# Down blocks of seven: one sum of weight quadrants by a transfer, and the last sums, transfers and two product chains in another order

## The chip, the cores and the metric

The kernel runs on one core of a Trainium2 chip. The metric is the device time of one execution in microseconds (us). The core's engines are TensorE (PE; its weight loads are listed apart as PEld), VectorE (DVE), ScalarE (ACT), GpSimd (POOL) and SyncE (SP). Each works through its own instructions in a fixed order and waits for the others by semaphores. Transfers are issued by SP, ACT or POOL and moved by 16 DMA engines. Matrix products go from SBUF to PSUM, whose banks ACT and DVE empty.

## The reference, cut to what matters

A decoder of two layers over 512 tokens of width 1024. Each layer has a mixing part and then a feed-forward part; only the latter is touched:

```
f = rmsnorm(h, ln_ffn_pre[layer])
f = (silu(f @ w_ffn_gate[layer]) * (f @ w_ffn_up[layer])) @ w_ffn_down[layer]
h = h + rmsnorm(f, ln_ffn_post[layer])
```

`w_ffn_gate` and `w_ffn_up` are 1024 x 2816, `w_ffn_down` is 2816 x 1024, all in f32. The inner width of 2816 is 22 tiles of 128.

## The kernel before, in words

**Three matmuls for one.** An f32 operand is split into a high part (a cast by ACT, `whi`) and a low part (source minus high part, by DVE, `wlo`); both happen in `split`, L239. `mm3` (L191 to L193) multiplies high by high, low by high and high by low into one PSUM bank. So each 128 x 512 piece of a weight costs one ACT and one DVE instruction before PE can use it.

**Seven products for eight.** The feed-forward part multiplies 2 x 2 blocks with seven products instead of eight (the scheme of Strassen and Winograd). The price is sums of quadrants, on DVE, ahead of the splits. `Seven` does it for gate and up: it loads two raw tiles of weights by SP (`loaded`, L144), makes four sums (`sums`, L1041, L1043, L1045, L1046), and seven products of 12 matmuls with 256 columns each, whose results are combined in the tiles x, a (`p`) and e (`q`). Product 7 uses the sum s3 and opens the bank e. `sevens` runs a gate seven and then an up seven, in the order of products 1, 7, 2, 6, 4, 3, 5. Only a layer's first pair goes another way.

**Groups.** After the first two tiles of the inner width (done plainly) come five groups of four: `groups = ((2, 6), (6, 10), (10, 14), (14, 18), (18, 22))`. In a group `sevens` runs twice (tiles m and m + 1 each). The first four groups end in a down block, `down_sevens`; the last one goes to `tail_of`. With two layers there are eight down blocks. PE works through block, gate, up, gate, up, block and so on.

**A down block** multiplies the group's four tiles of activations (two pairs, made by `Inner`, the x of each product) with a 2 x 2 block of `w_down` for each pair. `DownSeven` holds such a block's quadrants a11, a12, a21, a22. The pair's first one (`a` in `down_sevens`) is loaded into two raw tiles (L1194), out of the four that the sevens use too; in each, two quadrants lie side by side, so one quadrant is four pieces of 128 numbers in a partition. The second one (`b`) is spare: it has four tiles of its own (`wd`, L1188), loaded at the start of the second `sevens` of the group. `sums` makes s3 = a11 - a21 (L1205), the parts of a11, a21 + a22 (L1207) and a11 - a21 (L1208), all on DVE; product 3's weight is a further sum (L1220). Each product has 6 matmuls of 512 columns for each of a and b. They go to three pairs of banks: `chain` (tile yc, tag "tr"), `shared` (ys, "lg"), `lows` (yl, "mm"). The order is 1, 7, 2 of a; 1, 7 of b; then product 6 of both into the chain, 2 of b, 5 and 3 of both into the chain, and 4 of both into shared. After product 6 ACT copies the chain's bank into shared (L1256).

**Where the results go.** `ys[tb][dh]` are eight SBUF tiles (token block, half of the output). Some results are copied out by ACT into a tile yo (`put`, L1232) and added to ys by an accumulating transfer from POOL (L1234); some are added by DVE: lows into ys[x][0] (L1262), shared into ys[x][1] (L1265), the chain into ys[x + 2][0] (L1268). ys[x][1] gets one of each, so its sum by DVE waits for the transfer to land. POOL also issues the accumulating transfer that makes some of `Inner`'s low parts (`split_aside`, L1153).

**What sets the order.** The code is written as a flow of tiles. A planner, with its own model of costs, lays down each engine's order ahead of the run: among the instructions that it takes to be ready it picks by their order in the code, `tc.high_priority` raises some, and `tc.issue_after` (in `behind`) ties one behind another on its engine. So an instruction that stands later in the code may be laid ahead of one that stands earlier, but on the chip each engine keeps the order laid down and stands still at an instruction whose input isn't there. Buffers come from pools by tag, and a tile waits for a buffer's last reader.

Of the kernel before, what the change touches and what calls it, by code (L numbers as in the profile page):

```python
# [15 lines left out]
P = 128  # L16
# [24 lines left out]
def hybrid(ctx: ExitStack, tc: tile.TileContext, i: dict, out: bass.AP):  # L41
# [147 lines left out]
    def mm3(o, w, x, start, stop, more=False):  # L189

        PE.matmul(o, w[0], x[0], start=start, stop=False, skip_group_check=more)  # L191
        PE.matmul(o, w[0], x[1], start=False, stop=False, skip_group_check=more)  # L192
        return PE.matmul(o, w[1], x[0], start=False, stop=stop, skip_group_check=more)  # L193
# [891 lines left out]

    ended = [None]

    def sevens(pair, plain_first, opens=False):

        if not plain_first:  # L1090
            for make in pair:
                u = make()
                with behind(ended if opens else ()):
                    u.sums()
                opens = False
                for n in (1, 7, 2, 6, 4, 3, 5):
                    u.run(n)
                u.end()
            return
        us = []  # L1100
        for make in pair:
            us.append(make())
            us[-1].sums()
            for n in (1, 2, 3):
                us[-1].run(n)
        for some in ((7, 6), (4, 5)):
            for u in us:
                for n in some:
                    u.run(n)
        for u in us:  # L1110
            u.end()

    def feed_forward(layer, phase, xp, meanwhile=None):
# [68 lines left out]
        class DownSeven:  # L1182

            def __init__(self, k, spare):
                if spare:
                    self.a = [plain("wd").rearrange("p (m c) -> p m c", m=4) for _ in range(4)]
                    for n, a in enumerate(self.a):
                        last_load[0] = nc.sync.dma_start(  # L1188
                            a, i["w_down"][layer, 4 * (n // 2) : 4 * (n // 2) + 4, :, k + n % 2, :].rearrange("m p c -> p m c"))
                else:  # L1190
                    raws = []
                    for dh in range(2):
                        raw = wp.tile([P, 1024], F32, tag="raw", name=name("raw"), bufs=4)
                        last_load[0] = nc.sync.dma_start(  # L1194
                            raw.rearrange("p (m c) -> p m c", m=4),
                            i["w_down"][layer, 4 * dh : 4 * dh + 4, :, k : k + 2, :].rearrange("m p k c -> p m (k c)"))
                        raws.append(raw.rearrange("p (m k c) -> p m k c", m=4, k=2))
                    self.a = [r[:, :, x, :] for r in raws for x in range(2)]

            def sums(self, pair):  # L1200
                self.x = pair.x
                a11, a12, a21, a22 = self.a
                self.w = {2: a12, 4: a22}
                s3 = temp("s3").rearrange("p (m c) -> p m c", m=4)
                V.tensor_sub(s3, a11, a21)  # L1205
                self.w[1] = self.parts(a11)
                V.tensor_add(a21, a21, a22)  # L1207
                V.tensor_sub(a11, a11, a21)  # L1208
                self.w.update({5: a21, 6: a11, 7: s3})

            def parts(self, src, aside=False):
# [1 line left out]
                split_aside(src, *(t.rearrange("p (m c) -> p m c", m=4) for t in pair), aside)  # L1213
                return pair

            def product(self, outs, n, start, stop):
                w = self.w[n]
                if n == 2:
                    w = self.parts(w)
                    V.tensor_add(self.a[1], self.a[0], self.a[1])  # L1220
                    self.w[3] = self.a[1]
                elif n != 1:
                    w = self.parts(w)
                for x, o in enumerate(outs):
                    c = slice(x * P, (x + 1) * P)
                    mm3(o, tuple(t[:, c] for t in self.x[n]), w, start, stop, True)

        def down_sevens(us, pairs):

            def put(x, *where):  # L1230
                some = prob("yo")
                A.copy(some, x)  # L1232
                for tb, dh in where:
                    G.dma_start(ys[tb][dh], some, accum_op=ALU.add)  # L1234

            def both(outs, n):
                a.product(outs, n, False, False)
                b.product(outs, n, False, True)

            a, b = us  # L1240
            a.sums(pairs[0])
            chain, shared, lows = ([ps(t, s=n) for _ in range(2)] for t, n in (("tr", "yc"), ("lg", "ys"), ("mm", "yl")))
            a.product(chain, 1, True, False)
            a.product(shared, 7, True, False)
            a.product(lows, 2, True, False)
            b.sums(pairs[1])
            b.product(chain, 1, False, True)
            for x in range(2):
                put(chain[x], (x, 0))
            b.product(shared, 7, False, True)  # L1250
            for x in range(2):
                put(shared[x], (x, 1), (x + 2, 1))
            both(chain, 6)
            with tc.high_priority():
                for x in range(2):
                    A.copy(shared[x], chain[x])  # L1256
            b.product(lows, 2, False, True)
            both(chain, 5)
            for x in range(2):
                put(chain[x], (x + 2, 1))  # L1260
            for x in range(2):
                V.tensor_add(ys[x][0], lows[x], ys[x][0])  # L1262
            both(shared, 4)
            for x in range(2):
                V.tensor_add(ys[x][1], shared[x], ys[x][1])  # L1265
            both(chain, 3)
            for x in range(2):
                V.tensor_add(ys[x + 2][0], chain[x], ys[x + 2][0])  # L1268

        fs = [(act("fhi"), act("flo")) for _ in range(2)]  # L1270

# [14 lines left out]
        for tb in range(TB):  # L1286
            for dh in range(2):
# [2 lines left out]
                    token_products(o, fs[k], w[dh][k], tb, k == 0, k == 1)  # L1290
                A.copy(ys[tb][dh], o)

        for gi, (k0, k1) in enumerate(groups):
            fs, pairs, downs = [], [], []
            for m in range(k0, k1, 2):
                if meanwhile and m == k1 - 2 and gi == len(groups) - 1:
                    next(meanwhile)
                if gi < len(groups) - 1:
                    pairs.append(Inner(m < k1 - 2))
                    if m > k0:  # L1300
                        downs.append(DownSeven(m, True))
                else:
                    fs += [(act("fhi"), act("flo")) for _ in range(2)]
                sevens((lambda: Seven(xs, lambda n: i["w_gate"][layer, m + n], "mm", gate_rows),
                        lambda: Seven(xs, lambda n: i["w_up"][layer, m + n], "lg",
                                      lambda row, t: up_rows(row, t, fs, pairs and pairs[-1]))), m == 2, m == k0)
            nk = k1 - k0
            if gi == len(groups) - 1:
                if layer:
# [2 lines left out]
                if meanwhile:  # L1312
# [5 lines left out]
                V.tensor_scalar_mul(eps, eps, RMS_EPS)  # L1318
                return tail_of(fs, lambda kp, dh, aside, k0=k0: down_weights(layer, k0 + 2 * kp, dh, aside), ys, eps,
                               layer == 1)  # L1320
            down_sevens([DownSeven(k0, False)] + downs, pairs)


    def layer_b(phase, fp):
# [297 lines left out]
```

## Time and profile before

| | |
|---|---|
| time, median of 3 runs | 1107.38 us (1104.4 to 1107.46) |
| the profiled execution's time | 1104.82 us |
| its span, first to last instruction | 1103.1 us |
| mean granted clock of PE | 0.998 |
| busy: PE, PEld | 1082.6 us (98%), 983.3 us (89%) |
| busy: DVE, ACT, POOL | 970.7 us (88%), 754.5 us (68%), 93.8 us (9%) |
| DMA queues of SP and of POOL, share of 16 engines | 34.4%, 11.7% |

A line of the profile names engine, line of the code and tiles as output<-inputs, buffer numbers left out. A helper's line stands for all that call it, so L239 is every split; the tile tells them apart. A list of waits says which engine and line waited for which other: us in total, how often, the longest. Matmuls overlap, and one lasts longer (0.28 or 0.39 us) than the step from one start to the next. An event's line can name an earlier wait of its engine.

### The profile page before, as it was taken

To read this page: it belongs to the slowest core of one execution; us is meant where nothing else is said; L and a number is where in the kernel's file an instruction comes from. 1 tells how busy PE (TensorE), PEld (TensorE's weight loads), DVE (VectorE), ACT (ScalarE), POOL (GpSimd) and SP (SyncE) were. 2 spreads that over 40 slices of the span, in tenths; PEclk is the share of its full clock that TensorE was granted. 3 is DMA by queue.
4 is the path that set the end of the run, shared out by engine and by line. 5 is a ranking of instruction groups with operands and counts; after the bars stand their busy time and mean duration, and the time that the engine had idled before them with its cause. 6 is when DMAs were issued, how large, how long until landed. Compare 5 with 4: busy or idle time off the path is not lost.

```text
span 1103.1 us, 19756 instructions
## 1 busy us (share of the span) xinstructions
PE 1082.6 (98%) x7266; PEld 983.3 (89%) x7267; DVE 970.7 (88%) x1942; ACT 754.5 (68%) x1588; POOL 93.8 (9%) x120
## 2 busy tenths in 40 slices
PE   9999999999999999999999999999999999999998
PEld 7998889997979899998988998889997979899996
DVE  7879759998999999997968789868999989999986
ACT  7776578665756757677746788868666756756664
POOL 0000000002020201101000000000002020201100
PEclk9999999999999999999999999999999999999999
DMA  7521331338464664746222654531338464564722
GB/s 269 160 82 51 120 116 39 115 97 191 120 158 125 136 173 97 207 134 193 68 86 59 154 136 120 148 115 40 115 97 191 116 159 129 116 173 106 180 97 77
DMA packets 83992, 139.64 MB, mean 127 GB/s; under 512 B 6772, under 2 KB 49800, under 8 KB 83896
## 3 DMA queue, kind: packets, MB, share of 16 engines
q1 hardware_dynamic: 71480, 116.57, 34.4%
q0 software_dynamic: 11712, 21.50, 11.7%
q8 instruction: 57, 0.93, 0.4%
q10 hardware_dynamic: 704, 0.32, 0.1%
q14 instruction: 39, 0.32, 0.1%
HBM read 105.23 MB, written 2.10 MB: 97 GB/s over the span
## 4 chain that ended last, share of the span: by engine, by line
PE 85%; DVE 5%; DMA 5%; ACT 3%; issue 1%; SPq 1%; POOL 0%; DVEq 0%; ACTq 0%
PE a L193 5%; PE a L192 5%; PE a L191 5%; PE y L191 4%; PE y L193 4%; PE y L192 4%; PE ps L191 4%; PE ps L193 4%; PE ps L192 4%; DMA y<-yo 4%; PE e L193 3%; PE e L192 3%; PE e L191 3%; PE x L193 3%; PE x L192 3%; PE x L191 3%
## 5 line engine op out<-in xcount | busy, mean ns | idle before, releaser
L239 ACT CAST whi<-raw 128x512 fp32r<-128x512 f32 x444 | 260.7, 619 | 117.9 <-DVE raw L1045 58.2
L239 DVE TENSOR_TENSOR wlo<-raw,whi 128x512 fp32r<-128x512 f32 x444 | 290.6, 682 | 21.0 <-ACT whi L239 20.3
L193 PE MATMUL x<-xshi,wlo 128*128 128x256 f32 x320 | 90.4, 282 | 0.2 <-DVE wlo L239 0.2
L192 PE MATMUL x<-xslo,whi 128*128 128x256 f32 x320 | 90.1, 282 | 0.0
L191 PE MATMUL x<-xshi,whi 128*128 128x256 f32 x320 | 90.1, 282 | 0.0
L192 PE MATMUL a<-xslo,whi 128*128 128x256 f32 x320 | 89.9, 281 | 0.0
L191 PE MATMUL a<-xshi,whi 128*128 128x256 f32 x320 | 89.8, 281 | 0.0
L193 PE MATMUL a<-xshi,wlo 128*128 128x256 f32 x320 | 89.7, 281 | 0.0
L1234 POOL DMA_DIRECT2D y<-yo x64 | 55.5, 1143 | 196.9 <-ACT yo L1232 135.0
L191 PE MATMUL ps<-xshi,whi 128*128 128x256 f32 (+1 forms) x224 | 68.4, 306 | 0.0
L192 PE MATMUL ps<-xslo,whi 128*128 128x256 f32 (+1 forms) x224 | 66.7, 298 | 0.0
L193 PE MATMUL ps<-xshi,wlo 128*128 128x256 f32 (+1 forms) x224 | 66.3, 298 | 0.0
L239 ACT CAST whi<-s 128x512 fp32r<-128x512 f32 x56 | 34.7, 620 | 41.0 <-DVE s L1205 25.0
L193 PEld LDWEIGHTS x<-xshi,wlo 128*128 128x128 f32 x320 | 60.6, 189 | 0.4 <-DVE wlo L239 0.4
L191 PEld LDWEIGHTS a<-xshi,whi 128*128 128x128 f32 x320 | 60.2, 188 | 0.4
L192 PEld LDWEIGHTS a<-xslo,whi 128*128 128x128 f32 x320 | 60.2, 188 | 0.4
L192 PEld LDWEIGHTS x<-xslo,whi 128*128 128x128 f32 x320 | 60.5, 189 | 0.0
L191 PEld LDWEIGHTS x<-xshi,whi 128*128 128x128 f32 x320 | 60.5, 189 | 0.0
L193 PEld LDWEIGHTS a<-xshi,wlo 128*128 128x128 f32 x320 | 60.2, 188 | 0.0
L193 PE MATMUL e<-t3hi,wlo 128*128 128x256 f32 x160 | 45.7, 286 | 10.5 <-DVE wlo L239 10.5
L191 PE MATMUL y<-whi,mixedhi 128*128 128x512 f32 x128 | 51.3, 401 | 0.0
L192 PE MATMUL y<-wlo,mixedhi 128*128 128x512 f32 x128 | 50.6, 395 | 0.0
(352 smaller groups left out, 3637.4 us busy)
## 6 DMA issues: line engine op xcount, KB each, us to landing
raw<-in_w_gate SPq DMA_DIRECT2D x44, 512.0 KB, 3.7
raw<-in_w_up SPq DMA_DIRECT2D x44, 512.0 KB, 5.3
y<-yo POOLq DMA_DIRECT2D x64, 256.0 KB, 5.8
raw<-in_w_down SPq DMA_DIRECT2D x28, 512.0 KB, 4.6
raw<-in_w_out SPq DMA_DIRECT2D x16, 512.0 KB, 4.0
wd<-in_w_down SPq DMA_DIRECT2D x32, 256.0 KB, 8.8
flo<-s POOLq DMA_DIRECT2D x16, 256.0 KB, 5.1
raw<-in_w_b_q SPq DMA_DIRECT2D x8, 512.0 KB, 4.4
```

Of the source, the lines that this page charges most:

```text
L191: PE.matmul(o, w[0], x[0], start=start, stop=False, skip_group_check=more)
L192: PE.matmul(o, w[0], x[1], start=False, stop=False, skip_group_check=more)
L193: return PE.matmul(o, w[1], x[0], start=False, stop=stop, skip_group_check=more)
L239: last_parts[:] = A.copy(hi, src), (eng or V).tensor_sub(lo, src, hi)
L1234: G.dma_start(ys[tb][dh], some, accum_op=ALU.add)
```

## The change

It touches `sevens`, `DownSeven`, `down_sevens` and the loop over the groups.

- `DownSeven` issues, when it is made, an accumulating transfer from POOL that adds a22 to a21 inside SBUF. The DVE sum a21 + a22 is gone. s3 is now (a11 - new a21) + a22, made after that difference instead of first.
- The shared results' four transfers into ys go in the order ys[0][1], ys[1][1], ys[2][1], ys[3][1]; before, ys[2][1] was second.
- `both` (products 6, 5, 4, 3) prepares the weights of a and b, then does all matmuls of the first output, a's and b's, and then those of the second. Before, a's for both outputs came first.
- The last sums (the chain into ys[x + 2][0], shared into ys[x][1]) are returned as `rest` and made in the next group's gate seven, behind its product 2.

```diff
--- before.py
+++ after.py
@@ -1085,7 +1085,7 @@
 
     ended = [None]
 
-    def sevens(pair, plain_first, opens=False):
+    def sevens(pair, plain_first, opens=False, rest=None):
 
         if not plain_first:
             for make in pair:
@@ -1095,6 +1095,9 @@
                 opens = False
                 for n in (1, 7, 2, 6, 4, 3, 5):
                     u.run(n)
+                    if rest and n == 2:
+                        rest()
+                        rest = None
                 u.end()
             return
         us = []
@@ -1196,16 +1199,16 @@
                             i["w_down"][layer, 4 * dh : 4 * dh + 4, :, k : k + 2, :].rearrange("m p k c -> p m (k c)"))
                         raws.append(raw.rearrange("p (m k c) -> p m k c", m=4, k=2))
                     self.a = [r[:, :, x, :] for r in raws for x in range(2)]
+                G.dma_start(self.a[2], self.a[3], accum_op=ALU.add)
 
             def sums(self, pair):
                 self.x = pair.x
                 a11, a12, a21, a22 = self.a
                 self.w = {2: a12, 4: a22}
                 s3 = temp("s3").rearrange("p (m c) -> p m c", m=4)
-                V.tensor_sub(s3, a11, a21)
                 self.w[1] = self.parts(a11)
-                V.tensor_add(a21, a21, a22)
                 V.tensor_sub(a11, a11, a21)
+                V.tensor_add(s3, a11, a22)
                 self.w.update({5: a21, 6: a11, 7: s3})
 
             def parts(self, src, aside=False):
@@ -1213,7 +1216,7 @@
                 split_aside(src, *(t.rearrange("p (m c) -> p m c", m=4) for t in pair), aside)
                 return pair
 
-            def product(self, outs, n, start, stop):
+            def weights(self, n):
                 w = self.w[n]
                 if n == 2:
                     w = self.parts(w)
@@ -1221,21 +1224,30 @@
                     self.w[3] = self.a[1]
                 elif n != 1:
                     w = self.parts(w)
+                return w
+
+            def product(self, outs, n, start, stop):
+                w = self.weights(n)
                 for x, o in enumerate(outs):
-                    c = slice(x * P, (x + 1) * P)
-                    mm3(o, tuple(t[:, c] for t in self.x[n]), w, start, stop, True)
+                    self.one(o, x, n, w, start, stop)
+
+            def one(self, o, x, n, w, start, stop):
+                c = slice(x * P, (x + 1) * P)
+                mm3(o, tuple(t[:, c] for t in self.x[n]), w, start, stop, True)
 
         def down_sevens(us, pairs):
 
-            def put(x, *where):
+            def put(x, to):
                 some = prob("yo")
                 A.copy(some, x)
-                for tb, dh in where:
-                    G.dma_start(ys[tb][dh], some, accum_op=ALU.add)
+                G.dma_start(ys[to[0]][to[1]], some, accum_op=ALU.add)
+                return some
 
             def both(outs, n):
-                a.product(outs, n, False, False)
-                b.product(outs, n, False, True)
+                ws = [u.weights(n) for u in us]
+                for x, o in enumerate(outs):
+                    for u, w in zip(us, ws):
+                        u.one(o, x, n, w, False, u is b)
 
             a, b = us
             a.sums(pairs[0])
@@ -1248,8 +1260,9 @@
             for x in range(2):
                 put(chain[x], (x, 0))
             b.product(shared, 7, False, True)
+            both_sums = [put(shared[x], (x, 1)) for x in range(2)]
             for x in range(2):
-                put(shared[x], (x, 1), (x + 2, 1))
+                G.dma_start(ys[x + 2][1], both_sums[x], accum_op=ALU.add)
             both(chain, 6)
             with tc.high_priority():
                 for x in range(2):
@@ -1261,11 +1274,15 @@
             for x in range(2):
                 V.tensor_add(ys[x][0], lows[x], ys[x][0])
             both(shared, 4)
-            for x in range(2):
-                V.tensor_add(ys[x][1], shared[x], ys[x][1])
             both(chain, 3)
-            for x in range(2):
-                V.tensor_add(ys[x + 2][0], chain[x], ys[x + 2][0])
+
+            def rest():
+                for x in range(2):
+                    V.tensor_add(ys[x + 2][0], chain[x], ys[x + 2][0])
+                for x in range(2):
+                    V.tensor_add(ys[x][1], shared[x], ys[x][1])
+
+            return rest
 
         fs = [(act("fhi"), act("flo")) for _ in range(2)]
 
@@ -1290,6 +1307,7 @@
                     token_products(o, fs[k], w[dh][k], tb, k == 0, k == 1)
                 A.copy(ys[tb][dh], o)
 
+        rest = None
         for gi, (k0, k1) in enumerate(groups):
             fs, pairs, downs = [], [], []
             for m in range(k0, k1, 2):
@@ -1303,7 +1321,7 @@
                     fs += [(act("fhi"), act("flo")) for _ in range(2)]
                 sevens((lambda: Seven(xs, lambda n: i["w_gate"][layer, m + n], "mm", gate_rows),
                         lambda: Seven(xs, lambda n: i["w_up"][layer, m + n], "lg",
-                                      lambda row, t: up_rows(row, t, fs, pairs and pairs[-1]))), m == 2, m == k0)
+                                      lambda row, t: up_rows(row, t, fs, pairs and pairs[-1]))), m == 2, m == k0, m == k0 and rest)
             nk = k1 - k0
             if gi == len(groups) - 1:
                 if layer:
@@ -1318,7 +1336,7 @@
                 V.tensor_scalar_mul(eps, eps, RMS_EPS)
                 return tail_of(fs, lambda kp, dh, aside, k0=k0: down_weights(layer, k0 + 2 * kp, dh, aside), ys, eps,
                                layer == 1)
-            down_sevens([DownSeven(k0, False)] + downs, pairs)
+            rest = down_sevens([DownSeven(k0, False)] + downs, pairs)
 
 
     def layer_b(phase, fp):
```

## Prediction

> **What bounds the kernel now.** I read the engine table first, then what TensorE (PE) waits for, then each down block and the stretch behind it by itself, then the order of VectorE (DVE) at one block's end.
>
> The head of the page, then the lists of waits of PE and of DVE (engine, line, what it waited for: us in total, times, longest):
>
> ```profile
> span 1103.1 us, 19756 instructions
> PE 1082.6 (98%) x7266; PEld 983.3 (89%) x7267; DVE 970.7 (88%) x1942; ACT 754.5 (68%) x1588; POOL 93.8 (9%) x120
> ```
> ```profile
> PE e L193 <- DVE wlo L239: 10.5, 6, 2.4
> PE yc L191 <- ACT ys L1256: 2.5, 8, 0.3
> PEld e L193 <- DVE wlo L239: 11.8, 6, 2.6
> PEld yc L191 <- ACT ys L1256: 6.0, 8, 0.8
> DVE y L1265 <- DMA y<-yo: 9.0, 4, 3.5
> DVE y L1265 <- PE yc L193: 6.4, 3, 2.1
> ```
>
> PE is the bound, and little of its time is waiting. Two waits stand out, both at down blocks. Six times, product 7 (tile e) of the gate's first seven behind a block waits for a weight's low part from DVE: 10.5 us by the matmuls, 11.8 by the weight loads. And in each of eight blocks product 5 waits for ACT's copy out of the chain's bank. DVE itself stands 15.4 us ahead of L1265, the sum into ys[x][1].
>
> The stretches show why so small a wait of DVE reaches PE. A block is 20.4 us, what follows up to the next block 41.5 (columns: length, then busy time of PE, PEld, DVE, ACT, POOL, then granted clock, DMA share, GB/s):
>
> ```profile
> 242.10:262.80 20.70, 20.38 (x87) 15.39 (x86) 17.77 (x33) 13.70 (x26) 6.06 (x7) 1.00 0.64 135
> 306.40:326.80 20.40, 20.08 (x87) 15.49 (x85) 17.96 (x33) 13.50 (x26) 6.12 (x7) 1.00 0.64 136
> 326.80:368.30 41.50, 40.02 (x337) 39.81 (x336) 41.35 (x75) 26.59 (x55) 2.58 (x3) 1.00 0.54 150
> 906.40:949.20 42.80, 40.21 (x338) 39.80 (x337) 41.81 (x75) 26.60 (x55) 2.56 (x3) 1.00 0.53 145
> 264.90:267.40 2.50, 0.29 (x4) 0.08 (x2) 2.50 (x6) 2.05 (x5) 0.86 (x1) 1.00 1.13 243
> 268.70:272.10 3.40, 3.40 (x19) 3.40 (x18) 3.40 (x7) 1.20 (x3) 0.00 (x0) 0.50 0.56 161
> ```
>
> Behind the second block (306.4) DVE is busy for 41.35 of 41.5 us: it has no air to make up what it lost. Over that whole group it has 17.96 + 41.35 = 59.3 of 61.9 us, so 2.6 us idle. Where they lie is seen in DVE's timeline at the end of this block, and beside it at the end of the fourth (start, us, instruction, idle before it):
>
> ```profile
> 321.32 0.69 DVE L1041 TENSOR_TENSOR s<-raw,raw 128x512 f32<-128x512 f32 x1
> 321.93 0.69 DVE L239 TENSOR_TENSOR wlo<-raw,whi 128x512 fp32r<-128x512 f32 x1
> 322.53 0.69 DVE L1043 TENSOR_TENSOR raw<-raw 128x512 f32<-128x512 f32 x1
> 323.52 0.69 DVE L1265 TENSOR_TENSOR y<-ys,y 128x512 f32<-128x512 f32 x1 [0.30 <-PE ys L193]
> 326.35 0.69 DVE L1265 TENSOR_TENSOR y<-ys,y 128x512 f32<-128x512 f32 x1 [2.14 <-PE yc L193]
> 326.96 0.68 DVE L239 TENSOR_TENSOR wlo<-raw,whi 128x512 fp32r<-128x512 f32 x1
> 327.56 0.68 DVE L1045 TENSOR_TENSOR raw<-raw,raw 128x512 f32<-128x512 f32 x1
> 328.16 1.28 DVE L1268 TENSOR_TENSOR y<-yc,y 128x512 f32<-128x512 f32 x2
> 329.36 0.68 DVE L1046 TENSOR_TENSOR raw<-raw 128x512 f32<-128x512 f32 x1
> 329.96 0.68 DVE L239 TENSOR_TENSOR wlo<-s,whi 128x512 fp32r<-128x512 f32 x1
> ```
> ```profile
> 447.82 1.28 DVE L1265 TENSOR_TENSOR y<-ys,y 128x512 f32<-128x512 f32 x2
> ```
>
> One instruction follows the next by 0.60 us. Between the gate's first weight and the low part of its s3 (329.96), which product 7 needs, stand four final sums (L1265, L1268): 4 x 0.60 = 2.4 us, and 2.4 us of idle time ahead of them. In the fourth block both L1265 run together without a wait, and it is one of the two blocks (with the eighth) behind which PE has no wait at e. What the second L1265 waits for is a transfer, where the list of waits names one. POOL issues the sums into ys; its timeline, and the issues of transfers (KB each, median us to landing):
>
> ```profile
> 317.08 3.52 POOL L1234 DMA_DIRECT2D y<-yo  x4 [2.69 <-ACT yo L1232]
> ```
> ```profile
> y<-yo POOLq DMA_DIRECT2D x64, 256.0 KB, 5.8
> raw<-in_w_down SPq DMA_DIRECT2D x28, 512.0 KB, 4.6
> wd<-in_w_down SPq DMA_DIRECT2D x32, 256.0 KB, 8.8
> ```
>
> Four go out in a row from 317.08; ys[1][1]'s is the third of them, and the next group's wd loads move beside it.
>
> **The change, part by part.** The sum is made against the profiled execution's 1104.82 us, 2.6 under the median of three runs (1107.38) and near the fastest (1104.4).
>
> *Final sums behind product 2 of the next gate.* L1265 and L1268 leave the place ahead of s3. After L1043 (322.53) its low part then comes four instructions of 0.60 us later and ends near 325.6 instead of 330.6. The block ends at 326.8 and product 7 comes one product after that, so the wait at e goes in all six places: 10.5 to 11.8, I take 11.0. What is late next: the four sums now stand ahead of the low parts for products 6, 4, 3 and 5. They can start when the chain is done, near 326.9, and end at 329.3; product 6's low part is there at 329.9. Four sevens of seven products take PE 40.02 us, so 1.43 a product, and product 6 starts three products in, at 331.1. The cover is 1.2 us; without it, what exceeds it comes back in each block. Banks: the gate uses "mm", which L1262 has freed; the up seven wants the shared sums' "lg" some 10 us later.
>
> *The shared sums' transfers in another order.* ys[1][1]'s goes second instead of third. With the sums moved DVE stands in front of none of them, so I cost it at nothing; if a sum did meet an unlanded transfer, the 2.1 us of today would stand at the new place (rival 2).
>
> *a21 + a22 by a transfer.* Sixteen L1207 leave DVE: 16 x 0.60 = 9.6 us, 1.2 a group. None of it lies on PE's path while s3 is punctual; it is the air that keeps it so: 58.1 us of DVE against some 59.8 of PE (61.9 less today's waits) in a group. What it adds is two POOL issues a group, and a landing that L1208 waits for, with all of DVE's queue behind it:
>
> ```profile
> L390 POOL DMA_DIRECT2D memk<-memk x4 | 2.1, 542 | 46.5 <-DVE memk L388 46.5
> L1153 POOL DMA_DIRECT2D flo<-s x16 | 14.0, 873 | 264.4 <-ACT flo L1152 254.8 <-ACT s L1068 9.6
> DMA to landing us min/median/max: 3.3/5.8/11.3
> ```
> ```profile
> 221.63 5.62 SPq L1194 DMA_DIRECT2D raw<-in_w_down  x2
> 286.67 0.98 SPq L1194 DMA_DIRECT2D raw<-in_w_down  x2
> ```
> ```profile
> 300.92 0.68 DVE L1205 TENSOR_TENSOR s<-raw,raw 128x512 f32<-128x512 f32 x1
> ```
>
> (The third row is L1234's.) In a spare block (wd) a partition's row is whole, as in y<-yo: 0.87 us of POOL, 3.3 to 11.3 to land, and wd is loaded a group ahead; hidden. In raw the quadrant lies in four pieces a partition. 64 rows cost POOL 542 ns, 128 rows 873: 5 ns a piece, so 512 pieces are an estimated 2.8 us. Pieces of this size make wd's load 8.8 us for 256 KB where raw's takes 4.6 for 512: 3.8 times by the byte, so the transfer takes 3.3 to an estimated 3.8 x 3.3 = 12.6; I take 7, nearer to y<-yo's median as nothing else moves then. The load is issued by 287.7 and lands by 292.3. DVE comes to a at 300.9; product 7 (1.4 us behind the block's start, 306.4) needs L1208, s3, a cast and a low part, 2.5 us: the last moment is 305.3, 13.0 us after the load. In a layer's first block the second load is issued by 227.3 and lands by 231.9; the last moment is 242.1 + 1.4 - 2.5 = 241.0, room 9.1. With 7 it costs nothing; bounds nothing and 2 x 3.5 = 7. L1153, which may stand behind it on POOL, loses under 3 us, and its flo is first read in the block.
>
> *Both chains' products turn about.* In products 6, 5, 4 and 3 an output is done after six matmuls, half a product sooner, but the second pair's weights are wanted three matmuls sooner. At product 5 of the second block, PE and ACT:
>
> ```profile
> 317.62 0.39 PE L193 MATMUL yl<-whi,flo 128*128 128x512 f32 x1
> 318.34 0.50 PE L191 MATMUL yc<-whi,fhi 128*128 128x512 f32 x1 [0.32 <-ACT ys L1256]
> ```
> ```profile
> 317.16 0.63 ACT L239 CAST whi<-raw 128x512 fp32r<-128x512 f32 x1
> 317.68 1.08 ACT L1256 COPY ys<-yc 128x512 f32<-128x512 f32 x2
> ```
>
> Start follows start by 0.72, where 20.08 / 87 = 0.23 is the rule: 0.49 x 8 = 3.9 us lost. With chain[0] done 0.7 us sooner the copy can go ahead of ACT's cast; if ACT keeps its order nothing changes. Bounds 0 and 3.9; I take 2.0. Against it, PE may find the second pair's weights late, by 3 x 0.23 = 0.7 us at most: in 32 places 22 us. But at 321.32 DVE already serves the next gate with 5.5 us of the block to come, so products 4 and 3 are safe; I count product 6 and take 1.0, bounds 0 and 8 x 0.7 = 5.6.
>
> *The granted clock.* From 268.70 it is 0.50 for 3.4 us, so 1.7 us are lost, 1.3 us behind the first block's wait at e (264.9 to 267.4, PE busy 0.29 us). If the wait brings it about, it goes too; but the stretch from 906.4 has a wait as long (it is 1.3 longer than the one from 326.8) at full clock. The Trainium skill ("TensorE: Matmul & The Clock Gate", the clock gate) has the half clock follow an idle window of some 3.4 us; by that rule 2.5 us don't suffice, the stretch stays, and this term is 0. Bounds 0 and 1.7; I take 0.8.
>
> Sum: 11.0 + 2.0 + 0.8 - 1.0 = 12.8 us saved; 1104.8 - 12.8 = 1092. All gains at their upper ends and no cost: 11.8 + 3.9 + 1.7 = 17.4, so 1087.4.
>
> **Rivals.**
> 1. *DVE stays the bound.* If it stands 2.6 us a group as now, at the moved sums or at the landing, a group is 58.1 + 2.6 = 60.7 instead of 61.9 us: 1.2 x 6 = 7.2, so 1098. For it: 41.35 of 41.5. Against: what the sums need has landed at their new place.
> 2. *The wait only moves* from e to product 6: if the sums end more than the 1.2 us late in each block, most of the 11.0 returns and 2 to 3 are left, 1102. Against: the fourth block has its sums in today's place, without a wait, and PE has no wait at e.
> 3. *The transfer is late* (slower). Place: L1208 of a, all of DVE's queue behind it. It eats the 12.8 us and 3.3 more if each block loses 2.0, so from a landing of 13.0 + 2.0 = 15.0 us on: 1108 and over. For it: 11.3 was seen for whole rows. Against: 12.6 is the estimate's end.
> 4. *POOL's issues stop DVE.* Two a group would take 2 x 0.87 = 1.7 us, more than the 1.2 it is freed of: 0.5 more a group, and with today's waits 6 x 0.5 = 3 over before, 1108. The row on it:
>
> ```profile
> L239 DVE TENSOR_TENSOR wlo<-raw,whi x444: 626/682/696, 5.1 to 1078.0; 128x512 fp32r<-128x512 f32 x148
> ```
>
> The longest of these low parts took 696 ns against a median of 682, while 80 issues of POOL (64 + 16) fell among them. The Trainium skill ("SBUF — State Buffer", the shared port pair) has a DVE instruction with two SBUF inputs and a GpSimd read shut each other out for a whole instruction; by that rule rival 4 would hold, and the row doesn't show it.
>
> **How the numbers follow.** Forecast 0.66 (1087 to 1096), rival 1 0.17 (1096 to 1101), rival 2 0.07 (to 1105), rival 3 0.06, rival 4 0.04. About 0.3%, 3.3 us, can be told from no change. Faster takes the first two, 0.83; the same takes rival 2 and half of rival 4, 0.09; slower 0.08. The range of 8 in 10 runs from just under the bound of all gains, 1086, to the end of rival 1, 1101.
>
> **What would show it.** Right: no row for L1207's sum, sixteen more POOL issues; the wait of e for wlo under 2 us in all; the final sums behind s3's low part, without a wait; stretches behind a block near 40 us; product 5's weight loads waiting under 3 us for ACT. Wrong: DVE idle for a landing ahead of a11's difference; PE waiting for wlo at the gate's product 6 or 4, or at the chain's product 6; landings above 9 us from raw.

## The result, and the profile after

| | before | after |
|---|---|---|
| time, median | 1107.42 us (1104.4 to 1107.73) | 1092.84 us (1092.2 to 1094.33) |
| the profiled execution's time | 1104.82 us | 1094.33 us |
| busy: PE | 98% | 99% |
| ratio of times, 95% interval | | 0.9876 [0.9856, 0.9896] |

The change saves 14.6 us by the medians, 10.5 us between the two profiled executions. The one profiled of after is the slowest of its four.

The head of after's page, then its lists of waits of PE, PEld and DVE (engine, line, what it waited for: us in total, times, longest):

```profile
span 1092.6 us, 19871 instructions
PE 1081.0 (99%) x7267; PEld 983.3 (90%) x7267; DVE 964.6 (88%) x1926; ACT 755.1 (69%) x1588; POOL 110.3 (10%) x136
```
```profile
PE yc L191 <- ACT ys L1269: 2.9, 8, 0.4
PEld yc L191 <- ACT ys L1269: 6.4, 8, 0.8
PEld yc L191 <- ACT b L239: 2.9, 8, 0.8
DVE y L1275 <- DMA y<-yo: 4.3, 7, 1.6
```

PE's wait for the low part at e, 10.5 us in six places, has no row any more. Product 5's wait for ACT's copy (now L1269) is where it was: 2.9 us by the matmuls, 6.4 by the weight loads, against 2.5 and 6.0. DVE's 15.4 us ahead of the sum into ys[x][1] are gone from the lists too; what it still waits for a transfer into ys is 4.3 us at the lows' sum (L1275), where it waited 0.9 before (L1262).

The stretches (length, busy time of PE, PEld, DVE, ACT, POOL, granted clock, DMA share, GB/s): the first block, the second, what follows the second, and the start of the kernel:

```profile
243.60:264.70 21.10, 20.36 (x86) 15.50 (x85) 20.46 (x37) 15.65 (x30) 5.45 (x7) 1.00 0.63 129
304.50:324.80 20.30, 19.94 (x86) 15.43 (x85) 19.84 (x36) 15.73 (x30) 5.31 (x7) 1.00 0.65 133
324.80:364.70 39.90, 39.90 (x338) 39.88 (x337) 38.64 (x70) 24.37 (x51) 5.40 (x6) 1.00 0.67 171
9.20:12.60 3.40, 3.40 (x17) 3.30 (x17) 3.09 (x7) 2.69 (x6) 0.00 (x0) 0.50 1.02 409
```

Behind the second block PE is busy for 39.90 of 39.9 us, where it had 40.02 of 41.5. DVE has 38.64 there: 1.3 us of air instead of 0.15. The first block of a layer is 0.4 us longer than before, the others 0 to 0.1.

With all stretches measured so, the balance of the two profiled executions is: the six stretches behind blocks 1, 2, 3, 5, 6 and 7 are 13.7 us shorter (39.7 to 39.9 each; 10.5 to 11.8 of it the wait at e, by the rows of the matmuls and of the weight loads, 1.7 the half clock behind the first block, the rest small). Against that, the eight blocks are 1.2 us longer in all, the part ahead of the first block 1.5 (this execution has its half clock at 9.2 us, in the kernel's start), the middle 0.65; the tail is 0.2 shorter. 13.7 - 1.2 - 1.5 - 0.65 + 0.2 = 10.5. Without a half clock at its start, worth half of 3.4 us, it would have taken 1092.6, near the median.

DVE at the end of the second block, the counterpart of the row of instructions shown of before: the low parts of the gate's first weight and of s3, the first and the last of the four final sums, and what follows them (start, us, instruction; the lines between them are left out):

```profile
320.05 0.68 DVE L239 TENSOR_TENSOR wlo<-raw,whi 128x512 fp32r<-128x512 f32 x1
322.45 0.68 DVE L239 TENSOR_TENSOR wlo<-s,whi 128x512 fp32r<-128x512 f32 x1
323.66 0.68 DVE L1281 TENSOR_TENSOR y<-yc,y 128x512 f32<-128x512 f32 x1
325.62 0.68 DVE L1283 TENSOR_TENSOR y<-ys,y 128x512 f32<-128x512 f32 x1
326.22 2.48 DVE L239 TENSOR_TENSOR wlo<-raw,whi 128x512 fp32r<-128x512 f32 x4
```

s3's low part (322.45) now ends 1.7 us ahead of the block's end at 324.8 instead of 3.8 behind it. The four sums (L1281, L1283) run behind it from 323.66 on, with no idle time noted ahead of them, and the next low parts follow at once.

### The profile page after: what moved, and what is told of

It reads as the page before. It is cut to its first block, busy times and chain, and to the rows that moved or that the text cites. A ratio compares the mean times of both kernels' runs of the same rounds, so it can differ in the third digit from the quotient of the medians.

```text
span 1092.6 us, 19871 instructions
## 1 busy us (share of the span) xinstructions
PE 1081.0 (99%) x7267; PEld 983.3 (90%) x7267; DVE 964.6 (88%) x1926; ACT 755.1 (69%) x1588; POOL 110.3 (10%) x136
## 4 chain that ended last, share of the span: by engine, by line
PE 81%; DVE 7%; ACT 6%; DMA 4%; issue 2%; SPq 0%; ACTq 0%; POOL 0%; DVEq 0%; POOLq 0%
PE y L191 5%; PE y L192 5%; PE y L193 5%; PE a L193 4%; PE a L192 4%; PE a L191 4%; PE ps L191 4%; PE ps L193 4%; PE ps L192 4%; PE e L191 3%; PE e L193 3%; PE x L193 3%; PE x L192 3%; PE e L192 3%; PE x L191 3%; DVE wlo L239 2%
## 5 line engine op out<-in xcount | busy, mean ns | idle before, releaser
L239 DVE TENSOR_TENSOR wlo<-raw,whi 128x512 fp32r<-128x512 f32 x444 | 290.4, 683 | 21.3 <-ACT whi L239 20.7
L1243 POOL DMA_DIRECT2D y<-yo x48 | 40.9, 946 | 199.7 <-ACT yo L1242 138.1
L193 PE MATMUL y<-whi,mixedlo 128*128 128x512 f32 x128 | 50.3, 393 | 0.0
```

The lines of the kernel that those rows point to most:

```text
L239: last_parts[:] = A.copy(hi, src), (eng or V).tensor_sub(lo, src, hi)
L1243: G.dma_start(ys[to[0]][to[1]], some, accum_op=ALU.add)
```

## The experiments

Ratios are against the kernel before, measured on the same chip; its medians there were 1106.49 us (the first four kernels), 1106.17 (the next four) and 1106.57 (the last three). With 1107.42 above they differ by over 1 us, so differences of that size between medians of different groups mean little. At first my theory was the prediction's: the moved sums bring nearly all of it, and the quadrant sum's transfer is only air for DVE. The rivals were that one of the other parts had done it, or that all were needed together.

| kernel | median us | ratio, 95% interval |
|---|---|---|
| moved sums alone | 1090.90 | 0.9861 [0.9847, 0.9876] |
| quadrant sum alone | 1103.51 | 0.9968 [0.9956, 0.9980] |
| transfers' order alone | 1091.41 | 0.9865 [0.9852, 0.9877] |
| chains' order alone | 1107.87 | 1.0011 [0.9999, 1.0023] |
| after, sums in their old place | 1095.44 | 0.9904 [0.9890, 0.9918] |
| after, quadrant sum on DVE | 1090.55 | 0.9858 [0.9844, 0.9871] |
| after, old chains | 1092.47 | 0.9877 [0.9863, 0.9890] |
| after, b's product 2 behind product 6 | 1101.71 | 0.9960 [0.9947, 0.9974] |
| moved sums, transfers' order, half of that product behind | 1088.66 | 0.9837 [0.9823, 0.9852] |
| moved sums, two idle sums a group | 1092.80 | 0.9877 [0.9862, 0.9892] |
| moved sums, four idle sums a group | 1101.37 | 0.9955 [0.9942, 0.9968] |

### Before, with the moved sums alone

The diffs show the lines that matter ("..." stands for others).

```diff
+                    if rest and n == 2:
+                        rest()
...
-            for x in range(2):
-                V.tensor_add(ys[x][1], shared[x], ys[x][1])
             both(chain, 3)
-            for x in range(2):
-                V.tensor_add(ys[x + 2][0], chain[x], ys[x + 2][0])
+            def rest(): ...      # the same four sums
+            return rest
```

> Before, with the last sums moved behind product 2 of the next gate and nothing else of the change. Theory A (the four sums and their wait for a transfer stood ahead of s3's low part, and that alone made PE wait at e): the wait at e for wlo falls from 10.5 us to under 2, and 10 to 12 us of the change's 14.6 come, 1095 to 1098. Theory B (DVE is out of time as a whole, and the move only pays because the quadrant sum left DVE): half of the wait or more comes back at a later product, 1100 to 1105.

Measured: 1090.9 us, 1.9 less than the whole change and better than theory A's range. PE's row for the wait at e is gone. What follows the second block, and the whole group:

```profile
322.80:362.50 39.70, 39.70 (x337) 39.70 (x336) 39.57 (x72) 24.66 (x52) 2.58 (x3) 1.00 0.57 157
302.50:362.50 60.00, 59.67 (x422) 55.12 (x421) 59.24 (x107) 40.27 (x81) 8.70 (x10) 1.00 0.59 150
```

DVE does the work that it did before, 59.24 us a group (59.3 in the prediction), in 60.0 us instead of 61.9. No DVE work went; its idle time did, 2.6 us to 0.8. PE, at 59.67, is the bound again. The sums' relief through the transfer in SBUF isn't needed for that.

### Before, with the quadrant sum alone

```diff
+                G.dma_start(self.a[2], self.a[3], accum_op=ALU.add)
...
-                V.tensor_sub(s3, a11, a21)
                 self.w[1] = self.parts(a11)
-                V.tensor_add(a21, a21, a22)
                 V.tensor_sub(a11, a11, a21)
+                V.tensor_add(s3, a11, a22)
```

> Before, with a21 + a22 by a transfer and nothing else of the change. Theory A: the 9.6 us taken from DVE are not on PE's path, since DVE still stands at L1265 for the same transfer; the wait at e stays 8 us or more and the time within 0.3%, 1104 to 1108. Theory B: 1.2 us of DVE a group show in the time, 6 to 8 us, near 1100.

Measured: 1103.51 us, 3.0 us saved. The second group, and waits of PE, PEld and DVE:

```profile
302.40:363.60 61.20, 60.34 (x422) 55.21 (x421) 58.59 (x106) 39.77 (x80) 10.71 (x12) 1.00 0.65 155
```
```profile
PE e L193 <- DVE wlo L239: 1.0, 1, 1.0
PEld yc L191 <- ACT b L239: 6.3, 8, 0.8
PEld ys L191 <- DVE s L1080: 3.8, 8, 0.9
DVE y L1265 <- DMA y<-yo: 13.3, 9, 2.8
```

DVE's stall stayed: 13.3 us at the transfer, and 61.2 - 58.59 = 2.6 us idle a group. That is rival 1's formula, DVE's work plus 2.6. Still the wait at e is gone in all six places: 1.2 us less of work let DVE come out just in time there. (The 1.0 us that is left stands behind the eighth block, where before had none.) Much of what it brought was lost in the blocks, which are 0.9 us longer on average (21.0 to 21.7): the weight loads of the first products wait for a split by ACT (yc <- ACT b, 6.3 us) and for a sum of the activations (ys <- DVE s, 3.8). That this kernel would keep the wait at e is refuted; that it would gain little is not, though 1103.5 lies just under theory A's range.

### Before, with the shared transfers' order alone

```diff
-            for x in range(2):
-                put(shared[x], (x, 1), (x + 2, 1))
+            both_sums = [put(shared[x], (x, 1)) for x in range(2)]   # put now returns its tile
+            for x in range(2):
+                G.dma_start(ys[x + 2][1], both_sums[x], accum_op=ALU.add)
```

> Before, with ys[1][1]'s transfer issued second instead of third and nothing else. Theory A: that transfer lands some 1.5 us sooner, DVE's wait ahead of L1265 shrinks by as much in six blocks, and so does PE's at e: 4 to 8 us, 1099 to 1103, with the sums in their old place. Theory B: DVE's place for the sums, not the landing, decides, under 2 us.

Measured: 1091.41 us, as much as the moved sums, though the sums stand in their old place, and better than either theory allowed. DVE at the end of the second block, the four sums and s3's low part (lines between them left out):

```profile
319.67 1.39 DVE L1266 TENSOR_TENSOR y<-ys,y 128x512 f32<-128x512 f32 x2 [0.26 <-PE ys L193]
322.45 1.39 DVE L1269 TENSOR_TENSOR y<-yc,y 128x512 f32<-128x512 f32 x2 [0.20 <-PE yc L193]
324.36 0.68 DVE L239 TENSOR_TENSOR wlo<-s,whi 128x512 fp32r<-128x512 f32 x1
```

All four sums still stand ahead of s3's low part. But both into ys[x][1] (L1266) run together: the 2.14 us ahead of the second are gone because its transfer, now issued second, has landed. What is left of PE's wait at e:

```profile
PE e L193 <- DVE wlo L239: 0.3, 1, 0.3
```

So it was enough to end DVE's standing still for one transfer; the 2.4 us of work ahead of s3 could stay. It is not the only way: the moved sums ended the wait as well, and so did 1.2 us less of work with the stall kept. The wait was what stall and work together took over the time that PE left them.

### Before, with the chains' order alone

```diff
-                a.product(outs, n, False, False)
-                b.product(outs, n, False, True)
+                ws = [u.weights(n) for u in us]
+                for x, o in enumerate(outs):
+                    for u, w in zip(us, ws):
+                        u.one(o, x, n, w, False, u is b)
```

> Before, with both chains' matmuls in the new order and nothing else. The prediction's bounds: 2.0 us gained at product 5 and 1.0 lost at product 6. After the result: the wait at product 5 is unchanged (2.9 us by the matmuls against 2.5), so theory A: within 2 us of before, a block 0 to 0.1 us longer. Theory B: the new order costs the 0.1 to 0.4 us that a block got longer in the changed kernel, 1 to 2 us slower.

Measured: 1107.87 us, ratio 1.0011 [0.9999, 1.0023]: no change that can be told. Its waits of PE, and the wait at e with the stretch at half clock that follows, behind the first and behind the sixth block:

```profile
PE e L193 <- DVE wlo L239: 10.1, 6, 2.4
PE yc L191 <- ACT ys L1265: 2.5, 8, 0.3
```
```profile
264.00:266.40 2.40, 0.50 (x5) 0.29 (x4) 2.40 (x5) 1.87 (x5) 0.86 (x1) 1.00 1.16 264
266.80:270.20 3.40, 3.40 (x18) 3.40 (x17) 3.40 (x7) 2.21 (x5) 0.00 (x0) 0.50 0.57 114
909.20:911.60 2.40, 0.95 (x8) 0.96 (x9) 2.40 (x5) 2.40 (x6) 0.86 (x1) 1.00 0.56 98
911.90:915.30 3.40, 3.40 (x18) 3.40 (x17) 3.40 (x6) 1.30 (x3) 0.00 (x0) 0.51 0.65 166
```

Neither product 5's wait (2.5 us, as before) nor the order's feared cost shows. Both long waits at e are followed here by 3.4 us at half clock; before had one of the two.

### After, with one part taken back: sums, quadrant sum, chains

The first has the four sums in their old place again, the second a21 + a22 on DVE, the third the old order in `both`; the diffs are those above, reversed.

> The changed kernel with the last sums back in their old place (quadrant sum by transfer, transfers' order and chains as changed). Theory now (any one relief of about 1.2 us or more of DVE's time a group ends the wait at e: the moved sums and the earlier landing each did by themselves; the rest of the change adds nothing): 1091 to 1094, e under 1 us. Rival (the moved sums are what carries the changed kernel): e's wait back, over 1098.

> The changed kernel with a21 + a22 back on DVE. Theory now (the quadrant sum's new place costs a block 0.1 to 1 us, at the first products, and gives nothing where s3 is punctual anyway): 1090 to 1092, 1 to 2 us faster than the changed kernel, the matmul of product 1 on b without its 0.76 us step in the first blocks. Rival (DVE needs that air): slower than the changed kernel, 1095 and more.

> The changed kernel with both chains' products in the old order (all of a's matmuls, then b's). Theory now (the planner lays PE's order by readiness, and the order in the code moves little): within 1 us of the changed kernel, 1092 to 1094. Rival (the new order costs the 0.1 us that each block got longer, or product 5's wait is longer with it): 1 to 3 us faster.

Measured: 1095.44, 1090.55 and 1092.47 us. Where the sums stand is worth some 3 us once the other parts are there (2.6 by the medians, 3.1 by the ratios), though it is worth 15.6 alone; the time falls between the two theories' ranges. The first kernel's row of the wait at e, and DVE at the first sum into ys[x][1] of its eighth block:

```profile
PE e L193 <- DVE wlo L239: 2.1, 2, 1.6
1016.25 0.69 DVE L1275 TENSOR_TENSOR y<-ys,y 128x512 f32<-128x512 f32 x1 [1.89 <-DMA y<-yo]
```

One of the six waits remains without it, at 0.4 us (behind the sixth block). The other row, 1.6 us, is new: it stands behind the eighth block, where before had none, and DVE stands 1.89 us there for the first sum's transfer, so the new order of the transfers doesn't end that stall everywhere. Each of three parts ends most of the same wait, so their gains don't add. The quadrant sum makes the change slower. Without it the four runs take 1089.81 to 1090.83; with it, and the old chains, 1092.06 to 1093.15 on the same chip. The two differ in the chains' order too, but that makes no difference here either (1092.47 against 1092.84 for the whole change).

### After, with b's product 2 behind product 6

Product 5's wait stood at 2.5 to 2.9 us in all kernels so far. The timeline of after at that place, PE and then ACT (start, us, instruction, idle before it):

```profile
315.61 0.40 PE L193 MATMUL yc<-whi,flo 128*128 128x512 f32 x1
316.36 0.50 PE L191 MATMUL yc<-whi,fhi 128*128 128x512 f32 x1 [0.36 <-ACT ys L1269]
```
```profile
314.75 1.07 ACT L1242 COPY yo<-ys 128x512 f32<-128x512 f32 x2
315.71 1.08 ACT L1269 COPY ys<-yc 128x512 f32<-128x512 f32 x2
```

ACT begins its copy 0.1 us behind the start of the chain's last matmul; no cast stands ahead of it any more, but two copies into yo (L1242), without a gap. PE has nothing else to do meanwhile, because b's product 2 was laid ahead of the chain. So I tied that product behind product 6:

```diff
-            both(chain, 6)
+            end = both(chain, 6)
...
-            b.product(lows, 2, False, True)
+            with behind([end]):
+                b.product(lows, 2, False, True)
```

> The changed kernel with b's product 2 tied behind product 6 on PE, so that its six matmuls (1.4 us) stand between product 6 and product 5. Theory A (product 5 waits for ACT's copy of a bank that product 6 has only just left, and nothing of PE's is left to do meanwhile, as the planner has spent product 2 before): the start-to-start step of 0.76 us falls to 0.23, 0.5 us in eight blocks, 3 to 4 us, 1089. Rival (product 2 fills holes where it stands now, and product 6's weights are late without it): the wait moves to product 6, within 1 us of the changed kernel or slower.

Measured: 1101.71 us, 8.9 slower than after. Its waits of PEld:

```profile
PEld yc L191 <- ACT yo L1242: 7.0, 8, 0.9
PEld yc L191 <- ACT b L239: 5.8, 8, 0.8
PEld ys L191 <- DVE s L1080: 5.0, 8, 1.3
```

Product 5's wait is gone, and three others have come in its stead: with six matmuls less ahead of it, product 6 starts before ACT has emptied the chain's banks (yc <- ACT yo). The blocks are 21.5 to 22.6 us. The expectation's rival came true.

### The moved sums and the transfers' order, with half of that product behind

Three matmuls of the six are enough to cover 0.5 us, so only the second output's are tied; the quadrant sum stays on DVE, the chains in their old order.

```diff
-            b.product(lows, 2, False, True)
+            b.product(lows, 2, False, True, [end])   # in product, x == 1 alone is held
```

> Before with the moved sums and the transfers' new order, the quadrant sum on DVE and the chains in the old order, and of b's product 2 only the second output's three matmuls (0.7 us) tied behind product 6. Theory A (0.5 us a block is lost at product 5, and three matmuls are enough to cover it while the other three stay free to fill holes): 8 x 0.5 = 4 us faster than the moved sums alone, 1086 to 1088, no wait of yc for ACT's copy into ys. Rival (as with all six tied, the holes that product 2 filled open elsewhere in the block): blocks of 20.3 us or more, 1090 to 1094.

Measured: 1088.66 us (1088.45 to 1088.87), the best of all, 4.2 less than the whole change. The moved sums and the transfers' order together, with the new order of the chains, took 1090.55 (above), so it is the held matmuls that bring some 2 us, if the chains' order is worth nothing. The second block and what follows it:

```profile
302.20:322.30 20.10, 20.10 (x86) 15.34 (x85) 19.62 (x36) 15.37 (x30) 5.39 (x7) 1.00 0.65 134
322.30:362.10 39.80, 39.80 (x338) 39.78 (x337) 39.69 (x72) 24.95 (x52) 3.32 (x4) 1.00 0.57 158
```

A block after a layer's first is 20.03 to 20.15 us, from its first matmul to the first one behind it, where the moved sums alone have 20.25 to 20.33, and PE is busy for all of both stretches. The matmuls' wait for ACT's copy has no row any more, and the weight loads wait 2.3 us for it, where the moved sums alone had 6.0. So product 5's wait can be filled, though for about 2 us in all, not for the 3.9 that the prediction had as its upper end, nor for theory A's 4 (the time lies just above its range). Only 0.2 us a block, in six of eight blocks, are seen in the blocks themselves; the layers' first blocks are no shorter (21.1 us).

### The moved sums, with two and four idle sums a group

To measure DVE's room behind the block, idle DVE sums (bf16 into a tile that nobody reads; they add work and leave none out) were made behind the moved ones:

```diff
                         rest()
+                        for _ in range(2):           # 4 in the second kernel
+                            V.tensor_add(temp("junk", (P, T), "sq", 3, BF16), h[:, 0, :], h[:, 1, :])
```

> The moved sums alone, with two idle DVE sums of 512 columns (1.2 us) added behind them in each group. Theory A (a group lasts as long as DVE's work and idle time together wherever that is more than PE's 59.9 us; the moved sums alone have 59.2 and 0.8): 60.4 and what idle time is left, 0.5 to 1.2 us a group in six groups, 1094 to 1098. Theory B (only the wait for the landing ahead of s3 mattered, and DVE has room): within 1 us of the moved sums alone, 1091.

> The same with four idle DVE sums (2.4 us) a group. Theory A: 61.6 us of DVE and its idle time, 1.6 to 2.4 us a group in six groups, 1100 to 1106, and PE waiting for wlo. Theory B: the cover of 1.2 us at product 6 is used up twice over, at most 1.2 us a group, 1098.

Measured: 1092.8 and 1101.37 us. The first is inconclusive, and in neither theory's range: the planner laid six of a layer's eight idle sums into the stretch ahead of the first block and none into the second and third group. These two groups serve as the measure for the second kernel, which has two idle sums (1.28 us) in its second group and four (2.48 us) in its third. The two groups of the first kernel, then those of the second:

```profile
304.70:364.50 59.80, 59.53 (x422) 55.35 (x421) 59.30 (x107) 40.08 (x82) 8.69 (x10) 1.00 0.57 150
364.50:424.20 59.70, 59.42 (x422) 55.25 (x421) 59.15 (x107) 40.12 (x81) 8.69 (x10) 1.00 0.58 150
```
```profile
303.60:363.40 59.80, 59.53 (x422) 55.33 (x421) 59.18 (x107) 39.39 (x79) 8.68 (x10) 1.00 0.58 150
363.40:425.80 62.40, 60.77 (x422) 55.33 (x421) 62.11 (x111) 40.24 (x80) 8.71 (x10) 1.00 0.56 144
```

The group with two idle sums is no longer, but DVE did no more in it either, 59.18 us: it put other work off. Its first sum on wd for the block stands 1.3 us ahead of the block at the group's start (303.6) and 0.1 at its end (363.4):

```profile
302.26 0.68 DVE L1210 TENSOR_TENSOR s<-wd,wd 128x512 f32<-128x512 f32 x1
363.31 0.68 DVE L1210 TENSOR_TENSOR s<-wd,wd 128x512 f32<-128x512 f32 x1
```

So DVE fell behind by 1.2 us, and the next group pays: 62.4 us, 62.11 of them DVE. Both groups together take 122.2 us against 119.5; of 3.8 us added, 2.7 show and 1.1 are taken up, as much as DVE was idle in the two groups (0.5 and 0.55). That is theory A, whose range holds 1101.4 while theory B's 1098 is passed: DVE has about half a microsecond of room a group here, and the excess was put off by a group, not absorbed. Where PE then waits is not product 6: it waits 1.1 us at e in the last seven of the group, and the block in it is 21.3 us where it is 20.1 in the first kernel.

These two kernels have no wait for ACT's copy at product 5 either, though nothing is tied in them. The planner itself laid four matmuls of b's product 2 there, and a block of the first one takes 20.1 us. That bears out that such matmuls fill the wait.

## Why the prediction was right, point by point

**The wait at e (11.0 us): right in its size, too narrow in its cause.** All six waits went, 10.5 to 11.8 us of the 13.7. The prediction counted two things between the gate's first weight and s3's low part, 2.4 us of sums and 2.4 us of standing, and took away both by moving the sums. The transfers' order alone leaves the sums where they are and gains as much; it was costed at nothing, "with the sums moved", and so was right only as a part of the whole. The step to add was to ask whether the wait would survive if only one of the two halves went: it would not.

**What is late next (cover of 1.2 us at product 6): right that it holds, too small in size.** No wait for wlo came up at product 6. In after the sums begin ahead of the block's end, not behind it, and product 6's low part ends at 326.9; PE first uses it at 329.3, so the cover is 2.4 us. What limits DVE, by the kernels with idle sums, is not this cover but its idle time in a whole group.

**a21 + a22 by a transfer (hidden, 0): right for the landing, wrong for the sum.** DVE never stands for it. Its issues and landings in after, the spare blocks in the first row, the raw tiles in the second (ns of an issue: least, median, longest):

```profile
L1202 POOL DMA_DIRECT2D wd<-wd x8: 837/837/1047, 203.2 to 965.0; - x8
L1202 POOL DMA_DIRECT2D raw<-raw x8: 1290/1290/1316, 233.4 to 987.6; - x8
DMA to landing us min/median/max: 3.4/4.5/8.2
```

An issue for raw takes POOL 1.29 us where 2.8 were estimated by the piece, and everything has landed after 8.2 us where 13.0 were allowed, so rival 3 is out. Rival 2 is out as well, since no wait at product 6 has come up. What wasn't foreseen: with one DVE sum less and s3 made last, the planner laid the first products of the blocks anew, and PE meets them too early. Weight loads of yc wait 2.9 us for ACT's split and 2.6 for its copies into yo (2.2 and 0.6 with the quadrant sum on DVE). It costs about 1.9 us (1092.47 against 1090.55, if the chains' order is worth nothing), and the air that it was to give DVE wasn't needed, since PE was the bound without it. Which waits make up the 1.9 us stays open. The longer first blocks of a layer are not among them: with the quadrant sum on DVE they take 21.0 and 21.1 us too, the second of them here:

```profile
816.20:837.30 21.10, 20.34 (x86) 15.33 (x85) 20.64 (x37) 15.78 (x30) 5.34 (x7) 1.00 0.62 130
```

**Product 5's wait (2.0 us): the step that failed.** It took the copy to go ahead of ACT's cast once the chain is done sooner. The wait went from 2.5 to 2.9 us. With the chains' order alone ACT kept its order, the case that the prediction had put at nothing; its cast and its copy in the second block:

```profile
316.10 0.63 ACT L239 CAST whi<-raw 128x512 fp32r<-128x512 f32 x1
316.62 1.08 ACT L1265 COPY ys<-yc 128x512 f32<-128x512 f32 x2
```

In after two copies into yo stand in the cast's place. What ended the wait, in the kernel with half of b's product 2 behind, was matmuls for PE to put between.

**Cost of the chains' order (1.0 us at product 6): failed in its place.** The order costs nothing that can be told, by itself or within the change. The blocks did grow by 1.2 us in all, most of it in the first block of each layer, which is as long without the quadrant sum's transfer. So the terms that failed, 2.0 gained and 1.0 lost, come to a gain of 1.0 us against a loss of 1.2 us. Without the half clock in its start, after's profiled execution would be 10.5 + 1.7 = 12.2 us faster. That the forecast of 12.8 lies so near is in part luck: the 2.0 us counted in vain at product 5 came in behind the blocks, 1.0 us more than the 11.0 of the wait at e and 0.9 more than the 0.8 of the half clock.

**The half clock (0.8 us): the upper bound, 1.7, came true behind the first block.** No kernel without the long waits at e has one between the blocks. The four longest waits, windows of 2.4 to 2.7 us with PE busy for 0.3 to 1.0 us, two in before and two in the kernel with the chains' order, were followed by one in three cases. The Trainium skill ("TensorE: Matmul & The Clock Gate", the clock gate), weighed in the prediction, asks for an idle window of some 3.4 us; the rows show it behind shorter ones. The gain isn't in the profiled times, as after's profiled execution has one at its start. That before's wider spread (1103.4 to 1110.6, the moved sums alone 1090.5 to 1091.3) comes from it fits, but wasn't shown.

**Rival 1, DVE stays the bound (1098)**, has the idle time that the quadrant sum alone leaves, where the stall stays: 2.6 us a group. In after, PE is the bound. **Rival 4, POOL's issues stop DVE**, isn't seen:

```profile
L239 DVE TENSOR_TENSOR wlo<-raw,whi x444: 627/683/695, 4.7 to 1067.5; 128x512 fp32r<-128x512 f32 x148
```

With 136 instructions of POOL instead of 120, the longest low part takes 695 ns where it took 696. The rule that the prediction set beside this rival is about GpSimd reading SBUF; nothing here shows that issuing a transfer is such a read.

## What to carry to other kernels

Where an engine is busy for 96% of a group, one stall of 2.4 us in front of one transfer can be nearly the whole loss: before you take work off the engine, issue that transfer a place earlier, and count the gains of several cures for one wait only once. A wait that ends on the copy behind a chain is filled with matmuls held back for it, just as many as cover it: three gained 2 us; six, tried on the changed kernel, lost 9. When you load an engine to measure its room, check in the same window that its work has grown by as much: work put off into the next group looks like room. Taking an instruction away from one engine lets a planner lay another's order anew; look for the cost there, not only at the new transfer.

## What was not expected of the hardware

The granted clock of PE fell to 0.50 for 3.4 us behind windows of only 2.4 to 2.7 us in which PE was mostly idle, in three of four cases. The accumulating transfer within SBUF of 512 pieces cost POOL 1.29 us an issue, 0.45 us more than that of 128 whole rows (0.84): 1.2 ns for each further piece, where 5 ns had been worked out from 64 and 128 rows.
